# Split embedding weights kept in DRAM after the first pass, and new places for sums, transposes and loads, in a hybrid decoder step on one core

## The chip, the core and the metric

One Trainium2 chip, one core of it. The program works with five engines that each run their own list of instructions in order: TensorE (PE; PEld is its weight load), VectorE (DVE), ScalarE (ACT), GpSimd (POOL) and SyncE (SP), which here issues nearly every DMA. The metric is the device time of one execution in microseconds (us), as a median of several runs. Before the change it is 2644.22 us (three runs, 2639.54 to 2645.95).

## What is computed

One layer of a decoder for 2048 prompt tokens and 32 sample tokens (8 sequences of 4), all in float32, model width 1024:

```python
xn = rmsnorm(h, norm_mix);  proj = xn @ w_in                  # 1024 -> 3072, six groups of 512
o_a = rmsnorm(hgrn2_scan(...)) * silu(og)                     # 4 heads, 128x128 state each
z = conv31(ca * sigmoid(cg)) + bias                           # depthwise, 512 channels
o_b = silu(layernorm(z) * gain + bias)
h = h + concat(o_a, o_b) @ w_out
xn2 = rmsnorm(h, norm_ffn)
h = h + (silu(xn2 @ w_gate) * (xn2 @ w_up)) @ w_down          # inner width 2816
gate = sigmoid(rmsnorm(h, norm_ple) @ w_ple_gate)             # 1024 x 1024
h = h + gate * (p @ w_ple_proj)                               # 256 x 1024
y = rmsnorm(h, norm_final)
```

Outputs are y for prompt and sample, and the new scan and convolution states.

## The kernel before

**Numbers.** Every float32 matrix product is made of three TensorE products of a high and a low part: `wh*xl`, `wh*xh`, `wl*xh` (`mm3`, lines 541 to 544, and `mm3s`, 1630 to 1632). This text calls such three a triple. A weight piece of 128x512 is loaded as `raw`; ScalarE rounds it to `wh` (the helper `act`, shown as line 385), VectorE takes `wl = raw - wh` (the helper `tt`, line 390). `stt` (line 393) is the helper of operations with a scalar. Since helpers record them, nearly all VectorE rows carry lines 390 and 393 and are told apart by their tiles.

**Stages.** The mix stage (to about 945 us) goes over 8 blocks of 256 tokens: input norm, projections, scan, convolution, layer norm and output product, whose result h1 goes to DRAM (`h1d`). The second stage (`ffn`, 1920) goes over three passes of 696, 696 and 688 tokens, each of two halves (348 or 344 columns). A pass has 22 gate and up units `z` with Strassen's seven products for each (`strassen`, 1634; four of the seven weight combinations are kept in DRAM as `tch`/`tcl` by pass 0 and read by the others), six down stages `d`, and the embedding stage `p` (`embed`, 1863): 8 column tiles m with two weight pieces of the gate (`w_pg`) each and one piece of the projection (`w_pp`) for every two tiles. In the last pass the embedding goes over all eight tiles for half 0 and then again for half 1, so its pieces are loaded and split twice.

**Norms.** `rms2` (1287) makes a norm of one half: eight squares on ScalarE, eight sums on VectorE, one small memset (L1310), three transposes on TensorE (L1315), two reduces on VectorE (L1319, L1322), a power on GpSimd (`inverse_root`, shown as L426), and three transposes that spread the result (L1330). `norm2` is the norm before the ffn. Its `combine` (1371) takes the eight h1 columns of a pass two at a time per half (kp = 0 to 3): four loads and four scale operations, then the seven sums A12, A11, S1, A22, S2, S4, S3 that `strassen` multiplies with, in tiles `xa`/`x2`. kp = 3 ends last. `norm3` feeds the embedding together with `h2_split` (1935; tiles `xo`, `hx`), and `norm4` (1960) is the final norm: after its power, 16 scale operations (8 per half, L393 `h<-h,gn,px`) and the stores of y.

**Order.** `Sched.run` (188) writes all instructions in an order that it plans with estimated durations: for each engine the operation that can start first, then by a rank. A TensorE operation of any thread but the main ones (`lane`, `ffn`) that would have to wait is planned `SIDE` ns later, so that more products go ahead of it. Each engine, and SP's queue, then runs that list strictly in order on the chip. Buffers come from pools: `ring` (9 pairs of weight pieces, of which 4 hold the embedding's inputs, `pins`, through stage `p`), `raws`, `tmp2` (10 work tiles), `hres` (the residual of a pass), `main` (PSUM banks `pm`, with some `px`).

```python
                if e == "pe" and th[0].__name__ not in ("lane", "ffn") and s > self.clock[e]:
                    s += self.SIDE
```

## Time and profile before

| | |
|---|---|
| median of 3 runs | 2644.22 us |
| the profiled execution's own time | 2645.72 us |
| its span | 2644.0 us |
| mean granted TensorE clock | 0.98 of full speed |
| busy: PE / DVE / ACT / POOL | 96% / 75% / 41% / 5% |
| DMA: moved, mean rate | 470.86 MB, 178 GB/s |

The span is the time from the first to the last instruction; 1.7 us lie around it. A share of busy time is an average over the stages; where TensorE stands idle, and for whom, is read from its timeline and its waits. The granted clock has two levels, 1.00 (2.4 GHz) and 0.50 (1.2 GHz), and a stretch shows their mean.

### The profile page before, as it was taken

Reading aid. Unit: us, or ns where it says so; the run is one execution under the profiler, and the core shown is the slowest. Engines: PE = TensorE matmul, PEld = TensorE weight load, DVE = VectorE, ACT = ScalarE, POOL = GpSimd, SP = SyncE. Lnnn points to the kernel's source line nnn. Section 1 sums busy time; section 2 is a strip of 40 time slices with the busy share of each in tenths; the row PEclk is TensorE's granted clock in tenths of the full one; section 3 lists DMA queues with packets and bytes.
Section 4 is the critical chain, followed back from the end, with each engine's and each line's share of the span. In section 5 each row is a group of like instructions: output and inputs, shape, how many; then the busy total and the mean of one; then the engine's idle time right before and its main releaser. Section 6 shows DMA issues by size and latency. Waiting matters only on the chain.

```text
span 2644.0 us, 44170 instructions
## 1 busy us (share of the span) xinstructions
PE 2525.0 (96%) x15646; PEld 2368.0 (90%) x15646; DVE 1978.4 (75%) x4578; ACT 1082.1 (41%) x2477; POOL 140.4 (5%) x286
## 2 busy tenths in 40 slices
PE   7999999999999799999999899999998799999988
PEld 6987977778887699999999889999998799999977
DVE  8998899679886876666677857686587666677686
ACT  5553344334332343444354433343344334333353
POOL 0111010010110100000000000000000000000010
PEclk9999999999999799999999999999999899999999
DMA  8665646554546684565452374445622555554433
GB/s 310 222 211 187 236 159 199 197 179 162 165 139 204 201 278 164 187 211 177 159 207 74 128 255 169 154 161 192 216 81 96 163 193 195 196 173 162 148 95 118
DMA packets 290510, 470.86 MB, mean 178 GB/s; under 512 B 46576, under 2 KB 88048, under 8 KB 290288
## 3 DMA queue, kind: packets, MB, share of 16 engines
q1 hardware_dynamic: 287984, 466.63, 52.7%
q8 instruction: 123, 2.02, 0.3%
q10 hardware_dynamic: 2304, 1.41, 0.2%
q14 instruction: 99, 0.81, 0.1%
HBM read 368.27 MB, written 99.64 MB: 177 GB/s over the span
## 4 chain that ended last, share of the span: by engine, by line
PE 87%; DVE 6%; DMA 3%; POOL 1%; ACT 1%; issue 1%; SPq 0%; POOLq 0%; DVEq 0%; ACTq 0%
PE pm L1632 27%; PE px L1632 13%; PE pm L542 11%; PE pm L544 11%; PE pm L543 11%; PE px L544 2%; PE px L542 2%; PE px L543 2%; DVE h L390 1%; DVE wl L390 1%; PE pm L610 1%; PE pm L612 1%; PE pm L611 1%; DVE h L393 1%; POOL sm L426 1%
## 5 line engine op out<-in xcount | busy, mean ns | idle before, releaser
L390 DVE TENSOR_TENSOR wl<-raw,wh 128x512 fp32r<-128x512 f32 (+1 forms) x496 | 328.8, 667 | 151.8 <-ACT wh L385 138.9
L385 ACT ACTIVATE wh<-raw 128x512 fp32r<-128x512 f32 (+1 forms) x496 | 295.9, 608 | 309.4 <-PE pm L543 96.5
L542 PE MATMUL pm<-xal,wh 128*128 128x256 f32 (+2 forms) x960 | 324.0, 337 | 8.8 <-DVE xal L390 4.6
L544 PE MATMUL pm<-xah,wl 128*128 128x256 f32 (+2 forms) x960 | 311.1, 324 | 0.9 <-DMA wl<-wcl 0.9
L543 PE MATMUL pm<-xah,wh 128*128 128x256 f32 (+2 forms) x960 | 310.9, 324 | 0.0
L542 PE MATMUL pm<-xol,wh 128*128 128x348 f32 (+4 forms) x751 | 250.7, 334 | 9.2 <-ACT wh L385 5.2
L544 PE MATMUL pm<-xoh,wl 128*128 128x348 f32 (+4 forms) x751 | 246.4, 328 | 0.6 <-DVE wl L390 0.5
L543 PE MATMUL pm<-xoh,wh 128*128 128x348 f32 (+4 forms) x751 | 246.1, 328 | 0.0
L390 DVE TENSOR_TENSOR h<-pm,h 128x348 f32<-128x348 f32 (+1 forms) x335 | 172.5, 517 | 91.5 <-PE pm L544 42.6
L1632 PE MATMUL pm<-xal,wh 128*128 128x348 f32 (+1 forms) x707 | 228.6, 323 | 4.1 <-DVE h L390 1.8
L1632 PE MATMUL pm<-xah,wh 128*128 128x348 f32 (+1 forms) x707 | 227.6, 322 | 0.0
L1632 PE MATMUL pm<-xah,wl 128*128 128x348 f32 (+1 forms) x707 | 227.4, 322 | 0.1
L542 PEld LDWEIGHTS pm<-xal,wh 128*128 128x128 f32 x960 | 183.1, 191 | 36.0 <-issue 8.6
L393 DVE SCALAR_TENSOR_TENSOR t<-u,cvw,t 128x256 f32<-128x256 f32 x448 | 214.0, 478 | 0.0
L544 PEld LDWEIGHTS pm<-xah,wl 128*128 128x128 f32 x960 | 182.3, 190 | 15.8 <-DMA wl<-wcl 1.8
L385 ACT ACTIVATE wh<-tw 128x512 fp32r<-128x512 f32 x146 | 92.0, 630 | 249.7 <-DVE tw L390 92.9
L543 PEld LDWEIGHTS pm<-xah,wh 128*128 128x128 f32 x960 | 183.0, 191 | 11.7
L1632 PE MATMUL pm<-x2l,wh 128*128 128x348 f32 (+1 forms) x533 | 171.5, 322 | 6.1 <-DVE x2l L390 6.1
L426 POOL TENSOR_TENSOR sm<-sm,mhalf 128x2 f32<-128x2 f32 (+3 forms) x79 | 75.1, 952 | 1851.7 <-DVE sm L1322 1736.7
L393 DVE SCALAR_TENSOR_TENSOR h<-u,cvw,h 128x256 f32<-128x256 f32 x360 | 171.1, 476 | 2.2 <-ACT h L385 2.1
L1632 PE MATMUL pm<-x2h,wh 128*128 128x348 f32 (+1 forms) x533 | 171.7, 322 | 0.0
L1632 PE MATMUL pm<-x2h,wl 128*128 128x348 f32 (+1 forms) x533 | 171.7, 322 | 0.0
(292 smaller groups left out, 6513.7 us busy)
## 6 DMA issues: line engine op xcount, KB each, us to landing
raw<-w_gu SPq DMA_DIRECT2D x220, 256.0 KB, 3.2
wh<-wch SPq DMA_DIRECT2D x192, 256.0 KB, 2.8
wl<-wcl SPq DMA_DIRECT2D x192, 256.0 KB, 3.2
wh<-tch SPq DMA_DIRECT2D x176, 256.0 KB, 4.6
wl<-tcl SPq DMA_DIRECT2D x176, 256.0 KB, 4.8
raw<-w_dn SPq DMA_DIRECT2D x132, 256.0 KB, 3.2
tch<-wh SPq DMA_DIRECT2D x88, 256.0 KB, 2.8
tcl<-wl SPq DMA_DIRECT2D x88, 256.0 KB, 2.9
```

Source lines behind the costliest of these rows:

```text
L385: nc.scalar.activation(out, in_, func, scale=scale, bias=bias, **kw)
L390: return op("dve", d_tt(n), lambda: nc.vector.tensor_tensor(out=out, in0=a, in1=b, op=o), R, W)
L393: return op("dve", d_tt(n, not isinstance(s, float)), lambda: nc.vector.scalar_tensor_tensor(out=out, in0=a, scalar=s, in1=b, op0=o0, op1= ...
L426: return op("pool", 700.0, lambda: nc.gpsimd.tensor_tensor(out=s.ap[0:rows, out:out + n], in0=s.ap[0:rows, lo:lo + n], in1=mhalf[0:rows, 0 ...
L542: nc.tensor.matmul(out, lhsT=wh, rhs=xl, start=first, stop=False)
L543: nc.tensor.matmul(out, lhsT=wh, rhs=xh, start=False, stop=False)
L544: nc.tensor.matmul(out, lhsT=wl, rhs=xh, start=False, stop=last)
L610: nc.tensor.matmul(bank.ap, lhsT=xs[0], rhs=wl, start=(k == 0), stop=False)
L611: nc.tensor.matmul(bank.ap, lhsT=xs[0], rhs=wh, start=False, stop=False)
L612: nc.tensor.matmul(bank.ap, lhsT=xs[1], rhs=wh, start=False, stop=(k == KD - 1))
L1632: nc.tensor.matmul(out, lhsT=a, rhs=b, start=first and i == 0, stop=last and i == 2, skip_group_check=True)
```

## The change

1. **Kept embedding weights.** A new DRAM pair `pcache` (`pch`, `pcl`) has room for the 20 split pieces of stage `p`. In pass 0 each piece is split as before and then stored; passes 1 and 2 load the two parts from there into the ring pair instead of loading `raw` and splitting. `embed_tile` gives a pair back only after its store is issued. Passes 1 and 2 have 20 and 40 pieces.
2. **Final norm's transposes later.** `rms2` takes an event `late`, and `norm4` of passes 0 and 1 waits with its transposes until the next pass's first unit (half 0) or second unit (half 1) has its second product.
3. **Residual loads later.** `residual` for passes 1 and 2 starts after the second unit's second product.
4. **norm2 of the next pass earlier.** Its `combine` no longer waits for `norm3`'s rows.
5. **SIDE** becomes 4000 for norm2, norm3 and norm4, and stays 1000 for others.
6. **PN20** = 900 in place of 350: the rank of pass 0's norm2 and of its first two combines, whose work lies at the end of the mix stage beside the last block's convolution.

```diff
-    SIDE = 1000.0
+    SIDE = dict(norm2=4000.0, norm3=4000.0, norm4=4000.0)
...
-                    s += self.SIDE
+                    s += self.SIDE.get(th[0].__name__, 1000.0)
...
+    pcache = [dram.tile([20, 128, 512], F32, name="pc" + p) for p in "hl"]
...
     def residual():
         for t in PASSES:
+            if t:
+                yield wait(("zp", t, 0, 1, 1))
...
-    def rms2(n, get):
+    def rms2(n, get, late=None):
...
+        if late:
+            yield wait(late)
         bank = yield acq(misc)
...
     def norm2(t):
...
-            for h in HALVES:
-                yield wait(("r3", t - 1, h))
...
-            S.spawn(combine(t, kp, five), 350 if t == 0 and kp < 2 else 150 if t else 0)
+            S.spawn(combine(t, kp, five), PN20 if t == 0 and kp < 2 else 150 if t else 0)
...
-    S.spawn(norm2(0), 350)
+    S.spawn(norm2(0), PN20)
...
     def load2():
...
-                elif st[0] == "pin":
+                elif st[0] == "pin" or st[0] == "p" and t:
                     continue
...
+    def kept_name(key):
+        return key[:1] + key[2:-1]
+
+    def pkept(key):
+
+        at = 2 * key[2] + key[3] if key[0] == "p" else 2 * KD + key[2]
+        return [x[at] for x in pcache]
...
     def split2():
...
+                elif st[0] == "p" and t:
+                    for key, _ in plain(st, t):
+                        e = yield acq(ring)
+                        yield wait(("kept2", kept_name(key)))
+                        for x, part in zip(pkept(key), e):
+                            yield dma(part.ap.bitcast(F32), x, W=[part], nbytes=512 * 512)
+                        w2[key] = e
+                        S.fire(("w2", key))
...
+                        if st[0] == "p":
+                            S.spawn(keep_weights(pkept(key), e, ("kept2", kept_name(key))), 0)
...
     def embed_tile(t, m, hs):
...
         for a in range(2):
-            S.release(ring, w2.pop(("p", t, m, a, hs)))
+            key = ("p", t, m, a, hs)
+            yield wait(("kept2", kept_name(key)))
+            S.release(ring, w2.pop(key))
...
     def norm4(t, h):
         n = HALF[t]
-        bank = yield from rms2(n, of_res(t, h, "h3"))
+        bank = yield from rms2(n, of_res(t, h, "h3"), None if t == PASSES[-1] else ("zp", t + 1, 0, h, 1))
```

The new lines shift the helpers: in the orders of the change below, sums are line 392, scalar operations 395, `rms2`'s transposes 1321 and 1336, `mm3` 544 to 546, `mm3s` 1654 and the layer norm's last transposes 976.

**TensorE at the change from pass 0 to pass 1.** `px_181<-xah` (before) and `px_182<-xal` (now) are the first products of the new pass, `x2l` with them is the fourth column pair (kp = 3), `idn,f` and `idn,h` the final norm's first transposes, `idn,sm` the second ones. Before:

```order
L1632 MATMUL px_181<-xah,wl_81 128x348
L1315 MATMUL px_179<-idn,f_9125 128x128 x2
L1315 MATMUL px_179<-idn,f_9125 92x128
...
L1315 MATMUL px_182<-idn,f_9123 128x128 x2
...
L1330 MATMUL px_179<-idn,sm_67 128x128 x2
...
L1330 MATMUL px_182<-idn,sm_71 128x128 x2
...
L1632 MATMUL px_181<-x2l,wh_80 128x348
```

Now:

```order
L1654 MATMUL px_182<-xah,wl_81 128x348
L1654 MATMUL px_182<-x2l,wh_80 128x348
...
L1654 MATMUL pm_178<-x2l,wh_84 128x348
...
L1321 MATMUL px_183<-idn,h_77 128x128 x2
L1321 MATMUL px_183<-idn,h_77 92x128
L1654 MATMUL pm_180<-xal,wh_86 128x348
```

Before, both halves of the final norm stood ahead of the first product with kp = 3. Now that product follows the first three directly, and the transposes of half 0 come after the second group of four triples (six triples lie between its two transposes); half 1 follows in the second unit.

**VectorE at the same place.** `gn,r` are combine's scale operations, `gn,px` the final norm's 16, `x2l<-` the low parts of the sums of kp = 3; in the second excerpt `h_77,px_184`, `h_78` and `wl` belong to the embedding that ends (its last result, its residual sums, its last weights) and to the first weights of the new pass. Before:

```order
L393 SCALAR_TENSOR_TENSOR f_9124<-f_9124,gn,r_116 128x348
L393 SCALAR_TENSOR_TENSOR h_77<-h_77,gn,r_116 128x348
...
L393 SCALAR_TENSOR_TENSOR h_76<-h_76,gn,px_179 128x348 x3
L393 SCALAR_TENSOR_TENSOR h_79<-h_79,gn,px_179 128x348 x2
L393 SCALAR_TENSOR_TENSOR h_78<-h_78,gn,px_179 128x348 x3
L393 SCALAR_TENSOR_TENSOR h_76<-h_76,gn,px_182 128x348 x2
L393 SCALAR_TENSOR_TENSOR h_79<-h_79,gn,px_182 128x348 x3
L393 SCALAR_TENSOR_TENSOR h_78<-h_78,gn,px_182 128x348 x3
L390 TENSOR_TENSOR x2l<-f_9127,x2h 128x348
L390 TENSOR_TENSOR x2l<-h_77,x2h 128x348
```

Now:

```order
L395 SCALAR_TENSOR_TENSOR h_77<-h_77,px_184 128x348
L392 TENSOR_TENSOR wl_93<-raw_98,wh_92 128x512
L395 SCALAR_TENSOR_TENSOR h_78<-h_77,h_78 128x348
L392 TENSOR_TENSOR wl_97<-raw_102,wh_96 128x512
L395 SCALAR_TENSOR_TENSOR h_77<-h_77,gn,r_117 128x348
L392 TENSOR_TENSOR h_77<-h_77 128x348 x2
...
L392 TENSOR_TENSOR x2l<-h_77,x2h 128x348
...
L395 SCALAR_TENSOR_TENSOR h_76<-h_76,gn,px_181 128x348 x3
L395 SCALAR_TENSOR_TENSOR h_79<-h_79,gn,px_181 128x348 x2
L395 SCALAR_TENSOR_TENSOR h_78<-h_78,gn,px_181 128x348 x3
L392 TENSOR_TENSOR x2l<-h_77,x2h 128x348
```

Before, all 16 final scale operations stood between combine's last scale operation and A12 of kp = 3 (`x2l<-f_9127`). Now A12 (the first `x2l<-h_77`) comes ahead of them, seven VectorE instructions behind the embedding's last result (`h_77,px_184`), and eight of them stand ahead of S2 (`x2l<-h_77` at the end), which TensorE's fourth group of products needs. The same change of order is at the change from pass 1 to 2, where now all of kp = 3 but one sum is ahead of the last embedding operations.

**TensorE at the end of the mix stage.** `t` and `h_78` belong to the last block's scan and layer norm, `idn,h_77` and `idn,sm` to norm2 of pass 0, `pm<-xol` is the first output product. Before:

```order
L1205 MATMUL px_179<-idn,t_155 128x128 x2
L1207 MATMUL px_179<-idn,t_153 128x32
L1315 MATMUL px_179<-idn,h_77 128x128 x2
...
L1330 MATMUL px_180<-idn,sm_69 128x128 x2
...
L974 MATMUL px_179<-idn,h_78 128x128 x2
L974 MATMUL px_179<-idn,u_148 128x32
...
L974 MATMUL px_181<-idn,u_149 128x32
L542 MATMUL pm_177<-xol,wh_96 128x256
```

Now:

```order
L1209 MATMUL px_181<-idn,t_155 128x32
L1321 MATMUL px_182<-idn,h_77 128x128 x2
...
L1336 MATMUL px_181<-idn,sm_69 128x128 x2
...
L976 MATMUL px_184<-idn,h_78 128x128 x2
L976 MATMUL px_184<-idn,u_150 128x32
...
L976 MATMUL px_181<-idn,u_151 128x32
L1321 MATMUL px_184<-idn,h_77 128x128 x2
...
L1336 MATMUL px_182<-idn,sm_74 128x128 x2
...
L544 MATMUL pm_179<-xol,wh_96 128x256
```

Before, the transposes of norm2's half 0 came earlier, between the scan's products, and half 1's ahead of the layer norm's second set (`idn,h_78`, `idn,u`). Now half 0 is there, and half 1 stands between that set and the first output product.

## Rows read from the trace of the kernel before

**Rows 1.** The profile's page, busy time of each engine.
```profile
PE 2525.0 (96%) x15646; PEld 2368.0 (90%) x15646; DVE 1978.4 (75%) x4578; ACT 1082.1 (41%) x2477; POOL 140.4 (5%) x286
```

**Rows 2.** Stretches: busy us (instructions) per engine, granted clock, DMA share, GB/s.
```profile
1995.00:2075.00 80.00, 78.92 (x482) 78.50 (x481) 62.91 (x132) 36.26 (x76) 0.85 (x1) 0.97 0.35 114
2078.00:2104.00 26.00, 16.25 (x65) 14.63 (x66) 18.04 (x42) 5.86 (x13) 2.78 (x2) 0.67 0.55 165
20.00:30.00 10.00, 9.44 (x60) 8.35 (x60) 7.92 (x25) 5.53 (x16) 0.70 (x1) 1.00 1.06 405
```

**Rows 3.** Waits of TensorE: total us, times, longest us.
```profile
PE px L1330 <- POOL sm L426: 23.2, 9, 5.6
```

**Rows 4.** TensorE in time, change from pass 0 to 1: start, us, ..., [idle before].
```profile
1507.64 0.32 PE L1632 MATMUL px<-xah,wl 128*128 128x348 f32 x1
1511.17 0.99 PE L1315 MATMUL px<-idn,f 128*128 128x128 f32 x6 [3.21 <-DVE sm L1310]
1513.90 1.66 PE L1330 MATMUL px<-idn,sm 128*128 128x128 f32 x6 [1.74 <-POOL sm L426]
1526.18 0.66 PE L1632 MATMUL px<-x2l,wh 128*128 128x348 f32 x1 [10.62 <-DVE x2l L390]
```

**Rows 5.** VectorE in time, the same place.
```profile
1506.63 0.52 DVE L393 SCALAR_TENSOR_TENSOR f<-f,px 128x348 f32<-128x348 f32 x1 [0.43 <-PE px L544]
...
1517.81 7.88 DVE L393 SCALAR_TENSOR_TENSOR h<-h,gn,px 128x348 f32<-128x348 f32 x16
1525.61 0.52 DVE L390 TENSOR_TENSOR x2l<-f,x2h 128x348 fp32r<-128x348 f32 x1
```

**Rows 6.** TensorE in time, change from pass 1 to 2.
```profile
2078.70 0.90 PE L1315 MATMUL px<-idn,f 128*128 128x128 f32 x3 [4.51 <-DVE sm L1310]
...
2083.27 0.84 PE L1330 MATMUL px<-idn,sm 128*128 128x128 f32 x3 [2.59 <-POOL sm L426]
...
2096.78 0.66 PE L1632 MATMUL pm<-x2l,wh 128*128 128x344 f32 x1 [6.06 <-DVE x2l L390]
...
2119.55 0.55 PE L1632 MATMUL px<-xal,wh 128*128 128x344 f32 x1 [2.44 <-DMA wh<-tch]
```

**Rows 7.** TensorE in time, start of pass 1's embedding.
```profile
1990.70 0.84 PE L1330 MATMUL px<-idn,sm 128*128 128x128 f32 x3 [5.63 <-POOL sm L426]
1994.14 0.66 PE L542 MATMUL pm<-xol,wh 128*128 128x348 f32 x1 [2.59 <-ACT wh L385]
```

**Rows 8.** GpSimd in time, the same place.
```profile
1985.17 5.48 POOL L426 TENSOR_TENSOR sm<-sm,mhalf 128x3 f32<-128x3 f32 x1 [192.69 <-DVE sm L1322]
2001.94 0.85 POOL L426 TENSOR_TENSOR sm<-sm,mhalf 128x3 f32<-128x3 f32 x1 [11.29 <-DVE sm L1322]
```

**Rows 9.** VectorE in time, the same place.
```profile
1984.95 1.05 DVE L393 SCALAR_TENSOR_TENSOR xol<-h,gn,xoh 128x348 fp32r<-128x348 f32 x2
...
1988.88 1.06 DVE L393 SCALAR_TENSOR_TENSOR xol<-h,gn,xoh 128x348 fp32r<-128x348 f32 x2
```

**Rows 10.** TensorE in time, start of pass 2's embedding.
```profile
2549.32 0.84 PE L1330 MATMUL px<-idn,sm 128*128 128x128 f32 x3 [5.61 <-POOL sm L426]
2552.74 0.66 PE L542 MATMUL pm<-xol,wh 128*128 128x344 f32 x1 [2.58 <-ACT wh L385]
```

**Rows 11.** TensorE in time, end of the mix stage.
```profile
892.55 0.90 PE L1315 MATMUL px<-idn,h 128*128 128x128 f32 x3 [0.59 <-ACT hg L385]
897.41 0.84 PE L1330 MATMUL px<-idn,sm 128*128 128x128 f32 x3 [3.96 <-POOL sm L426]
```

**Rows 12.** VectorE in time, the same place.
```profile
898.78 0.58 DVE L393 SCALAR_TENSOR_TENSOR h<-h,gn,r 128x348 f32<-128x348 f32 x1 [0.61 <-ACT r L385]
```

**Rows 13.** Groups on VectorE, 1995 to 2075 us: count | busy, mean ns | idle.
```profile
L390 DVE TENSOR_TENSOR wl<-raw,wh 128x512 fp32r<-128x512 f32 x23 | 15.7, 689 | 5.5 <-ACT wh L385 5.5
```

**Rows 14.** Groups on ScalarE, 1995 to 2075 us.
```profile
L385 ACT ACTIVATE wh<-raw 128x512 fp32r<-128x512 f32 x21 | 13.0, 627 | 19.5 <-PE pm L543 11.8 <-issue 4.9 <-PE px L543 2.0
```

**Rows 15.** DMA issues of the page: count, KB each, median us to landing.
```profile
wh<-tch SPq DMA_DIRECT2D x176, 256.0 KB, 4.6
```

More of the change, by code (lines that the diff above doesn't have):

```diff
@@ L63 @@
 PSQ = 0
+PN20 = 900
 RANK = {"o": -2.0}
@@ L1901, in embed_tile @@
         if m % 2:
-            S.release(ring, w2.pop(("pp", t, m // 2, hs)))
+            key = ("pp", t, m // 2, hs)
+            yield wait(("kept2", kept_name(key)))
+            S.release(ring, w2.pop(key))
     def embed_evac(t, m, h, gate, proj):
```

## The prediction

> **What bounds the kernel now.** I read the page's busy shares first, where only TensorE is near full, 96% [rows 1], then stretches of the trace, then the waits of TensorE, then its timeline wherever it stops. In the middle of a pass's embedding TensorE works 78.92 of 80 us at a granted clock of 0.97 [rows 2], while VectorE and ScalarE have air: TensorE sets the time there, and work taken off the others is worth nothing by itself. Time is to be had only where TensorE stands. Its waits name the second transposes of a norm, for the power on GpSimd: 23.2 us in nine waits, 5.6 the longest [rows 3]. The timeline puts these waits, and longer ones, at the seams. From pass 0 to 1 it stands 3.21, 1.74 and 10.62 us, the last for VectorE's low part of a sum [rows 4]; VectorE was then in sixteen final scale operations, 7.88 us long, ahead of that sum [rows 5]. From pass 1 to 2 it stands 4.51, 2.59 and 6.06 us, and 2.44 for a weight load [rows 6]. At the start of the embedding of pass 1 it stands 5.63 us for the power and 2.59 for ScalarE's rounding of a weight [rows 7], at that of pass 2 5.61 and 2.58 [rows 10]. At the end of the mix stage it stands 3.96 us for a power [rows 11]. Each stop also brings the clock down: 2078 to 2104 us has a mean of 0.67 [rows 2].
>
> **The change part by part.** The sum is made against the profiled execution's own 2645.7 us (2644.0 of span and 1.7 around it), which is 1.5 above the median of the runs.
>
> *Split pieces no longer made (60 of them).* Each saves VectorE 0.689 us [rows 13] and ScalarE 0.627 [rows 14], some 40 and 38 us in all. TensorE is full there, so this counts nothing. If that cover were gone, only the four waits of the two embedding starts would show it. In place of the raw loads come 120 part loads, and 40 stores in pass 0. In pass 2 a tile of one half has ten triples of products; 482 instructions in 78.92 us [rows 2] are 0.164 each, so a tile takes 4.9 us and needs 2.5 pieces of two 256 KB parts, 1.31 MB, or 267 GB/s. The core has moved 405 GB/s in a stretch [rows 2]. Nothing is added for it; the bound above is rival 3. The added wait of `embed_tile` for the kept copy stands behind stores issued some us after the split, while the pair is still in use: nothing.
>
> *First weights of the embedding.* Passes 1 and 2 no longer wait for ScalarE's rounding: −2.59 and −2.58 [rows 7, 10]. The parts can be loaded long before, since half of the ring is free by then. Between norm3's first and second transposes now stand four triples in pass 1 and five in pass 2 instead of three; they fill 0.5 and 1.0 us of the waits of 5.63 and 5.61. The rest of these waits I leave: the power itself took 5.48 us [rows 8] beside ten VectorE operations that run from 1984.95 to 1989.94 [rows 9], and 0.85 where VectorE was quiet [rows 8]; in the new order nine of the ten still follow the norm's reduces. Sum of the two places −6.7; bounds 0 (a late load takes the rounding's place) and −16 (the powers go at 0.85 too).
>
> Here a rule and a row part. The Trainium skill, page "SBUF — State Buffer", section "Who interferes with whom", says that an operation of VectorE with two SBUF inputs and a GpSimd operation that reads SBUF exclude each other, and that the loser blocks until the other's instruction is finished. By that rule the power would lose one operation and then go, and the wait would not depend on how many follow. The trace disagrees: the power ended only with the series. By the row the two waits stay, by the rule they would go with any change of order; that is rival 2.
>
> *Pass 0 to 1.* The three waits, 15.6 us, go: the first product with kp = 3 no longer stands behind both halves of the final norm. Next in line is A12 itself. Behind the embedding's last result, which VectorE took at 1506.63 [rows 5], stand seven operations; with the durations of [rows 5, 12, 13] these are 0.52 + 0.69 + 0.52 + 0.69 + 0.58 + 1.04 + 0.52 = 4.6 us, with starts overlapping by 0.05 a piece as the sixteen do (7.88/16 = 0.49 [rows 5]) about 4.2, so A12 is there at 1510.9. TensorE wants it behind its third triple, at 1507.8 [rows 4]: a new wait of 3.1. The second is S2, which TensorE wants one triple after norm4's second transposes while VectorE starts eight scale operations then: 8 × 0.49 + 0.5 for the sum's low part − 0.5 to 0.9 for that triple, about 3.6. Norm4's chain from its first transposes to its second takes 4.9 − 0.9 = 4.0 us [rows 11]; six triples cover 2.9, the remaining 1 and the second half's like wait fall into these two. Each stop costs half-clock products behind it: 2 more. −15.6 + 3.1 + 3.6 + 2 = −6.9; bounds −15.6 (the scale operations move behind S2's need) and 0 (the sums come so late that TensorE stops as long as before).
>
> *Pass 1 to 2.* Here the order has all but one sum of kp = 3 ahead of the last embedding operations. Gone: 4.51 + 2.59 + 6.06 [rows 6], and 2.44 for the weight load, since the residual's loads that were queued ahead of it start two units later: 15.6. The half clock: 26 us at a mean of 0.67 hold 17.2 at half speed [rows 2]; the three stops there take 13.2 of the 26, so between 4.0 and 12.8 us of work went at half speed and cost 2.0 to 6.4; I take 4, the middle. Against it norm4's chain of 4.0 beside 2.9 of products, for two halves: between 0 and 2.2, taken as 1.5. −15.6 − 4 + 1.5 = −18.1; bounds −20 and −9.
>
> *End of the mix stage.* Half 1 of norm2 now has its whole chain between the layer norm's last transposes and the first output product, with no product in between. One such chain runs from 892.55 to 898.25, 5.7 us [rows 11]; half 0 takes the place half 1 had. Combine, which began at 898.78 [rows 12], begins some 8 us later; its sums then leave the front of the last convolution's VectorE work, at 0.5 each. I take +6, the chain alone; bounds 0 (the sums given back pay for it) and +12 (two chains in series).
>
> Residual loads later, and `SIDE`, have no term beyond these places. Sum: −6.7 − 6.9 − 18.1 + 6 = −25.7, so 2620.0 on the profile's scale and **2618.5** on the median's.
>
> **The rivals.** *1. The seams give little.* Pass 0 to 1 gains nothing (S2 takes the place of A12), the mix end costs its upper bound of 12, pass 1 to 2 keeps its weight wait of 2.44 and half of the clock's share, 14, and a load eats 1.7 of the embedding starts' gain, 5: 0 + 12 − 14 − 5 = −7, 2637. For it: eight scale operations do stand ahead of S2, and the norm's chain is longer than the products laid over it. Against it: at the change to pass 2 the order is clean. That the change doesn't do what it says, as to TensorE's order, is part of this. *2. The powers go quickly.* If one VectorE operation is all that holds a power up, or the new order leaves a hole for it, it takes 0.5 + 0.85 = 1.4 us in place of 5.48, and with the products between the transposes 4.5 more are won at each of two places: 2618.5 − 9 = 2609. Against it stand [rows 8, 9]. *3. Slower: the ring starves in pass 2.* Four of nine pairs hold the embedding's inputs, so five circulate in the first half of pass 2, two tiles' worth. A pair given back must be filled within about 2 × 4.9 = 9.8 us; from a landing of 9.8 on TensorE stops every two tiles, four times in eight tiles, by what is over. The loads of kept parts in the ffn land in 4.6 (median) [rows 15]. At a landing of 19.3 the four stops are 38 us: 2656, slower than before. It needs four times the landing seen; stores of y in the same queue speak a little for it.
>
> **How the numbers follow.** Forecast 0.65, rival 1 0.18, rival 2 0.12, rival 3 0.05. A measurement of this kernel tells some 0.3% from no change, 7.9 us, 2636.3 to 2652.1. The forecast's own terms run from about −45 to −5 at their ends together, but not all at one end; I give it 2607 to 2632. With rival 2 the range reaches down to 2600, with rival 1 up to 2637. Faster: forecast, rival 2 and half of rival 1, which lies at the bound: 0.65 + 0.12 + 0.08 = 0.85; same: the rest of rival 1, 0.10; slower: 0.05.
>
> **What would show it.** Right: TensorE's waits for `x2l` at the change to pass 1 are two of some 3 us instead of one of 10.6; at the change to pass 2 no wait over 2 us; no wait of the embedding's first product for ScalarE, but still 4.5 to 5.2 for the power; a first output product some 6 us later at the end of the mix stage. Wrong: a wait on `wh` or `wl` for a DMA within the embedding of pass 2 (rival 3); a power under 2 us at an embedding's start (rival 2); a wait of 7 us or more for S2 (rival 1).

## The result, and the profile after

The changed kernel takes 2628.84 us (median of 4 runs, 2628.53 to 2631.96) beside 2645.01 of the kernel before (4 runs). The ratio is 0.9946, interval 0.9929 to 0.9963: faster by 0.5%, some 14 us (16 by the two medians). The forecast was 2618.5 within 2600 to 2637, so sign and range hold, and the gain is little more than half of the 26 us that were summed. The profiled execution has a span of 2630.2 us, 13.8 shorter than before.

The page of the changed kernel, busy time of each engine, against [rows 1]:

```profile
PE 2525.8 (96%) x15646; PEld 2371.2 (90%) x15646; DVE 1938.9 (74%) x4518; ACT 1048.0 (40%) x2417; POOL 136.8 (5%) x286
```

TensorE is as busy as before; what changed is idle time and clock. Its waits (total us, times, longest us) beside [rows 3]:

```profile
PE px L1336 <- POOL sm L428: 16.3, 6, 4.4
...
PE pm L544 <- DVE h L392: 7.8, 1, 7.8
...
PE pm L1654 <- DVE x2l L392: 4.4, 1, 4.4
...
PE px L1654 <- DVE x2l L392: 4.2, 1, 4.2
PE pm L1654 <- DMA wh<-tch: 4.2, 1, 4.2
```

The one wait of 10.6 us for `x2l` is two of 4.4 and 4.2, as was expected (at 3.6 and 3.1). The waits for a norm's power sank from 23.2 us in nine to 16.3 in six. A wait of 7.8 for an output product's bank and one of 4.2 for a kept weight part are new in size. Two stretches (busy us and count of PE, PEld, DVE, ACT, POOL; granted clock; DMA share; GB/s):

```profile
2078.00:2104.00 26.00, 26.00 (x171) 25.92 (x171) 19.82 (x45) 9.53 (x19) 1.70 (x2) 1.00 0.83 269
1500.00:1550.00 50.00, 41.45 (x232) 40.68 (x232) 34.37 (x75) 17.60 (x37) 1.49 (x1) 0.86 0.61 199
```

The stretch 2078 to 2104 us, which had 16.25 us of products at a clock of 0.67 [rows 2], is now full at 1.00. The change from pass 0 to 1 still has holes.

To place the gain, the trace is cut at instructions that every version has: the first gate product, the last embedding product of pass 0, the first and the last product of the embeddings of passes 1 and 2, the last instruction of TensorE. Times in us:

| stretch | before | changed | difference | in the forecast |
|---|---|---|---|---|
| start to first gate product | 959.30 | 970.28 | +11.0 | +6 |
| pass 0 to its last embedding product | 547.23 | 547.18 | −0.1 | 0 |
| from there to pass 1's embedding | 475.55 | 470.27 | −5.3 | −6.9 |
| pass 1's embedding | 90.71 | 90.73 | 0.0 | −3.1 |
| from there to pass 2's embedding | 467.94 | 454.05 | −13.9 | −18.1 |
| pass 2's embedding | 89.36 | 83.63 | −5.7 | −3.6 |
| tail | 6.14 | 6.08 | −0.1 | 0 |
| sum | 2636.24 | 2622.22 | −14.0 | −25.7 |

How far such a stretch differs between traces of the same order is seen from the experiments below: the first one is 959.3, 959.8, 957.4, 962.0 and 958.3 us in the five versions with the old order at the mix stage's end, and 965.4 to 971.6 in the nine with the new one, means 959.4 and 968.3. So by the traces the new order costs some 9 us there, and 2 or 3 of the 11 lie within what one trace differs from another.

**The change from pass 0 to 1,** on TensorE and (second fence) on VectorE, beside [rows 4, 5]; the columns are start, us, engine, line, operation, tiles, shape, count and, in brackets, the idle time before and what ended it:

```profile
1523.06 0.66 PE L1654 MATMUL px<-x2l,wh 128*128 128x348 f32 x1 [4.16 <-DVE x2l L392]
...
1536.44 0.66 PE L1654 MATMUL pm<-x2l,wh 128*128 128x348 f32 x1 [4.39 <-DVE x2l L392]
```

```profile
1518.71 0.51 DVE L395 SCALAR_TENSOR_TENSOR h<-h,px 128x348 f32<-128x348 f32 x1
...
1522.49 0.51 DVE L392 TENSOR_TENSOR x2l<-h,x2h 128x348 fp32r<-128x348 f32 x1
...
1531.97 3.98 DVE L395 SCALAR_TENSOR_TENSOR h<-h,gn,px 128x348 f32<-128x348 f32 x8
1535.87 0.51 DVE L392 TENSOR_TENSOR x2l<-h,x2h 128x348 fp32r<-128x348 f32 x1
```

The embedding's last result is taken at 1518.71, A12's low part at 1522.49, and TensorE starts with it at 1523.06 after 4.16 us. Then eight final scale operations take 3.98 us, S2's low part comes right behind them at 1535.87, and TensorE goes on at 1536.44 after 4.39. Both waits are those of the forecast (3.1 and 3.6), by the same rows of VectorE. The last scale operation ahead of A12 started at 1521.00, as its load landed (1520.97), so the place of the loads bounds it too (experiment 9).

**The embedding of pass 1,** TensorE, GpSimd and VectorE, beside [rows 7 to 9]:

```profile
1996.52 0.84 PE L1336 MATMUL px<-idn,sm 128*128 128x128 f32 x3 [3.39 <-POOL sm L428]
...
2011.78 0.51 PE L1336 MATMUL px<-idn,sm 128*128 128x128 f32 x3 [2.09 <-POOL sm L428]
```

```profile
1991.50 4.96 POOL L428 TENSOR_TENSOR sm<-sm,mhalf 128x3 f32<-128x3 f32 x1 [194.08 <-DVE sm L1328]
2009.48 2.25 POOL L428 TENSOR_TENSOR sm<-sm,mhalf 128x3 f32<-128x3 f32 x1 [13.02 <-DVE sm L1328]
```

```profile
1994.69 1.06 DVE L395 SCALAR_TENSOR_TENSOR xol<-h,gn,xoh 128x348 fp32r<-128x348 f32 x2
...
2007.78 0.58 DVE L395 SCALAR_TENSOR_TENSOR f<-f,gn,r 128x344 f32<-128x344 f32 x1 [3.24 <-DMA f<-h1d]
2008.27 0.41 DVE L1325 TENSOR_REDUCE sm<-px 128x2 f32<-128x256 f32 x1
...
2009.03 0.28 DVE L1328 TENSOR_REDUCE sm<-px 92x1 f32<-92x128 f32 x1
...
2010.51 0.50 DVE L392 TENSOR_TENSOR h<-h,f 128x344 f32<-128x344 f32 x1
```

No product waits for ScalarE's rounding here any more; the first one waits 0.63 us for its kept part, the third 0.57. The wait for the power of the first half is 3.39 us in place of 5.63, but there is now a second wait for a power, 2.09 us, for the norm's second half. Behind it stand two rows of VectorE: a scale operation of combine for the next pass waited 3.24 us for its load, with the reduces of the norm (2008.27, 2009.03) queued behind it; and the sums of that combine ran beside the power, which took 2.25 us in place of 0.85.

**The change from pass 1 to 2,** first SyncE's queue (issues of one kind in a row are one line: start, us, count), then TensorE, beside [rows 6]:

```profile
2089.36 5.06 SPq L473 DMA_DIRECT2D y<-h  x9
2094.53 0.40 SPq L473 DMA_DIRECT2D raw<-w_gu  x1
2095.02 4.26 SPq L473 DMA_DIRECT2D y<-h  x9
...
2117.25 2.88 SPq L473 DMA_DIRECT2D y<-h  x6
...
2122.20 0.43 SPq L473 DMA_DIRECT2D wh<-tch  x1
```

```profile
2127.22 0.65 PE L1654 MATMUL pm<-xal,wh 128*128 128x344 f32 x1 [4.15 <-DMA wh<-tch]
```

All waits of the old order for VectorE and GpSimd are gone, the one for the weight load is not: 4.15 us in place of 2.44. From 2089 to 2122 us the queue issues 40 stores of y in eight groups, which take it 19.8 us (three of the groups are shown), some 0.5 each; a part issued at 2122.20 is what lands when TensorE's wait ends.

The same stretch has a second new wait at its far end, and the embedding of pass 2 behind it one for the power that is shorter than before (5.61 [rows 10]); TensorE:

```profile
2528.06 0.53 PE L1654 MATMUL pm<-xol,wh 128*128 128x344 f32 x1 [2.22 <-DVE h L392]
...
2540.02 0.51 PE L1336 MATMUL px<-idn,sm 128*128 128x128 f32 x3 [3.00 <-POOL sm L428]
```

The wait of 2.22 us, in the last down stage, is for a bank that VectorE empties at 2527.50, behind the low parts of the embedding's inputs. It is there, with 2.2 to 2.3 us, in every version with kept embedding weights and in none without them.

**The end of the mix stage,** TensorE and VectorE, beside [rows 11, 12]:

```profile
896.52 0.84 PE L1336 MATMUL px<-idn,sm 128*128 128x128 f32 x3 [4.41 <-POOL sm L428]
...
905.51 0.88 PE L1321 MATMUL px<-idn,h 128*128 128x128 f32 x3 [4.91 <-DVE sm L1314]
908.03 0.84 PE L1336 MATMUL px<-idn,sm 128*128 128x128 f32 x3 [1.64 <-POOL sm L428]
...
933.52 0.58 PE L544 MATMUL pm<-xol,wh 128*128 128x256 f32 x1 [7.80 <-DVE h L392]
```

```profile
925.74 0.95 DVE L392 TENSOR_TENSOR xal<-h,xah 128x348 fp32r<-128x348 f32 x2 [0.56 <-ACT xah L387]
...
931.69 0.95 DVE L392 TENSOR_TENSOR xal<-h,xah 128x348 fp32r<-128x348 f32 x2 [0.56 <-ACT xah L387]
...
933.05 0.75 DVE L392 TENSOR_TENSOR h<-h,pm 128x256 f32<-128x256 f32 x2
```

Half 1's transposes wait 4.91 us more and its power 1.64, and then an output product waits 7.80 us (4.04 before) for a bank that `h<-h,pm` at 933.05 has to empty. That operation stands in VectorE's list behind combine's second set of sums (925.74 to 932.64), which now begin later.

### The profile page after: what moved, and what is told of

The parts are those of the page before. It is cut to its first block, busy times and chain, and to the rows that moved or that the text cites. A ratio compares the mean times of both kernels' runs of the same rounds, so it can differ in the third digit from the quotient of the medians.

```text
span 2630.2 us, 44193 instructions
## 1 busy us (share of the span) xinstructions
PE 2525.8 (96%) x15646; PEld 2371.2 (90%) x15646; DVE 1938.9 (74%) x4518; ACT 1048.0 (40%) x2417; POOL 136.8 (5%) x286
## 4 chain that ended last, share of the span: by engine, by line
PE 87%; DVE 5%; DMA 4%; ACT 2%; POOL 1%; issue 1%; SPq 0%; POOLq 0%; DVEq 0%; ACTq 0%
PE pm L1654 28%; PE px L1654 12%; PE pm L544 11%; PE pm L546 10%; PE pm L545 10%; PE px L546 2%; PE px L544 2%; PE px L545 2%; DVE h L392 1%; PE pm L612 1%; PE pm L614 1%; PE pm L613 1%; DMA wl<-wcl 1%; DVE wl L392 1%; PE px L1136 1%; DMA h<-h1d 1%
## 5 line engine op out<-in xcount | busy, mean ns | idle before, releaser
L392 DVE TENSOR_TENSOR wl<-raw,wh 128x512 fp32r<-128x512 f32 (+1 forms) x436 | 287.6, 663 | 148.0 <-ACT wh L387 142.2
L387 ACT ACTIVATE wh<-raw 128x512 fp32r<-128x512 f32 (+1 forms) x436 | 258.9, 606 | 276.7 <-PE pm L545 90.6
L544 PE MATMUL pm<-xol,wh 128*128 128x348 f32 (+4 forms) x721 | 240.8, 334 | 8.4 <-DVE h L392 7.8
L1654 PE MATMUL pm<-xal,wh 128*128 128x348 f32 (+1 forms) x734 | 238.2, 325 | 9.2 <-DMA wh<-tch 4.2
L546 PE MATMUL pm<-xoh,wl 128*128 128x348 f32 (+4 forms) x721 | 236.6, 328 | 1.3 <-DMA wl<-pcl 1.3
L1654 PE MATMUL pm<-xah,wl 128*128 128x348 f32 (+1 forms) x734 | 236.8, 323 | 0.0
L545 PE MATMUL pm<-xoh,wh 128*128 128x348 f32 (+4 forms) x721 | 236.3, 328 | 0.0
L1654 PE MATMUL pm<-x2l,wh 128*128 128x348 f32 (+1 forms) x566 | 182.7, 323 | 4.4 <-DVE x2l L392 4.4
L1654 PE MATMUL pm<-x2h,wh 128*128 128x348 f32 (+1 forms) x566 | 182.9, 323 | 0.0
L1654 PE MATMUL pm<-x2h,wl 128*128 128x348 f32 (+1 forms) x566 | 182.6, 323 | 0.0
```

Of the source, the lines that this page charges most:

```text
L387: nc.scalar.activation(out, in_, func, scale=scale, bias=bias, **kw)
L392: return op("dve", d_tt(n), lambda: nc.vector.tensor_tensor(out=out, in0=a, in1=b, op=o), R, W)
L544: nc.tensor.matmul(out, lhsT=wh, rhs=xl, start=first, stop=False)
L545: nc.tensor.matmul(out, lhsT=wh, rhs=xh, start=False, stop=False)
L546: nc.tensor.matmul(out, lhsT=wl, rhs=xh, start=False, stop=last)
L1654: nc.tensor.matmul(out, lhsT=a, rhs=b, start=first and i == 0, stop=last and i == 2, skip_group_check=True)
```

## The experiments

All times are medians; a ratio is against runs of the kernel before on the same chip (medians 2645.97 to 2646.83).

**1. The old order at the end of the mix stage.**

```diff
-PN20 = 900
+PN20 = 350
-    SIDE = dict(norm2=4000.0, norm3=4000.0, norm4=4000.0)
+    SIDE = dict(norm3=4000.0, norm4=4000.0)
```

> The changed kernel with PN20 = 350 and norm2's SIDE at 1000, so that the end of the mix stage has the order that it had before; all else as changed. Theory: the first gate and up product came 11.0 us later after the change (970.28 against 959.30 us), and all of that is this order; the wait of 7.80 us for an output product's bank falls to some 4, and the kernel to 2617 to 2619 us. Rival: the later start of combine bought something behind it, in pass 0; then the first product is back at 959 but the time falls by under 6 us, to 2623 or more.

2625.64 us, ratio 0.9923 (0.9910 to 0.9937), against 0.9946 of the changed kernel: some 6 us by the ratios and 3 by the medians, less than expected and a time that the rival named. TensorE there:

```profile
896.84 0.84 PE L1336 MATMUL px<-idn,sm 128*128 128x128 f32 x3 [3.94 <-POOL sm L428]
...
923.35 0.39 PE L544 MATMUL pm<-xol,wh 128*128 128x256 f32 x1 [4.31 <-DVE h L392]
```

The bank wait is back at 4.31, and the first gate product at 959.80, 10.5 us earlier. Pass 0 is no longer than before (546.70), so nothing was bought there; the stretches behind pass 0 are 4.2 us longer together, 0.5 to 1.5 each, although every engine's order is the same there. So the rival's reason falls: the later start of combine bought nothing in pass 0, and behind it nothing is ordered otherwise. The price of part 6 and of norm2's part of part 5 is 9 us by the traces' first stretch and 3 to 6 by the times; that it is a price and no gain is shown, its size only so far.

**2. norm4's scale operations behind S3.**

```diff
         bank = yield from rms2(n, of_res(t, h, "h3"), ...)
+        if t != PASSES[-1]:
+            yield wait(("x2", t + 1, KP - 1, "S3"))
         for m in range(KD):
```

> The changed kernel, in which norm4 of passes 0 and 1 holds its sixteen scale operations back until the last sum (S3) of kp = 3 is made. Theory: the second wait at the change from pass 0 to 1 (4.39 us, for S2's low part) is the eight scale operations ahead of it on VectorE; it falls under 1.5 us, the first (4.16, A12) stays, and the kernel takes 2623 to 2625 us. Rival: S2 is late because the whole chain of sums behind A12 is late; the wait stays over 3 us and the time at 2627 to 2630.

2623.18 us, ratio 0.9919 (0.9905 to 0.9933), a time that the theory named, and the wait that it named:

```profile
1520.12 0.66 PE L1654 MATMUL px<-x2l,wh 128*128 128x348 f32 x1 [4.50 <-DVE x2l L392]
...
1530.10 0.43 PE L1654 MATMUL pm<-x2l,wh 128*128 128x348 f32 x1 [0.51 <-DVE x2l L392]
```

The A12 wait stays (4.50), the S2 wait is 0.51. In this trace the stretch to pass 1's embedding is 470.21 us, no shorter than the changed kernel's 470.27: a wait of 2.25 us for a weight part comes at 1570. Sixteen stores of y are issued until 1546.4 there, with TensorE 3 us ahead, and until 1539.8 in the changed kernel; that they make this load late was not tested. The place of the S2 wait is shown. Where the 5 us of the medians come from is not: in the trace 2.4 us lie in the first stretch, whose order is that of the changed kernel, 1.2 in pass 1's embedding and 1.1 on the way to pass 2's.

**3. The stores of y on ScalarE's queue.**

```diff
-            if t == PASSES[-1] and m % 2:
+            if t != PASSES[-1] or m % 2:
```

> The changed kernel, in which the stores of y of passes 0 and 1 are issued by ScalarE's queue instead of SyncE's. Theory: the wait of 4.15 us for a kept weight part early in pass 2 (2127 us) is SyncE's queue: stores of y, 0.43 us each to issue, stand ahead of the weight loads; without them the wait falls under 1 us and the kernel takes 2623 to 2625 us. Rival: the load is late in the memory, or behind residual loads; the wait stays over 3 us and the time at 2627 to 2631.

2647.55 us, ratio 1.0007 (0.9998 to 1.0016): the whole gain is lost, 8.7 us of it on the way to pass 1's embedding and 7.3 on the way to pass 2's. The wait for the weight part is gone, and this has come in its place, on TensorE and on ScalarE (ACTq is its queue):

```profile
2113.64 0.66 PE L1654 MATMUL pm<-xal,wh 128*128 128x344 f32 x1 [8.10 <-ACT h L387]
```

```profile
2103.45 4.77 ACTq L2003 DMA_DIRECT2D y<-h  x6
2108.26 0.46 ACT L387 ACTIVATE f<-px 128x344 f32<-128x344 f32 x1 [4.26 <-DMA y<-h]
2108.82 4.26 ACTq L2003 DMA_DIRECT2D y<-h  x6
2113.12 0.46 ACT L387 ACTIVATE h<-pm 128x344 f32<-128x344 f32 x1 [4.41 <-DMA y<-h]
```

An issue holds ScalarE's list some 0.4 us, and longer where the store waits for its data; single activations, which TensorE waits for, stand between groups of six. The miss says how costly these stores are where they stand in one burst, but not yet that they are what made the load late on SyncE.

**4. norm2 waits for norm3's rows again (part 4 undone).**

```diff
                     yield wait(("pin", t - 1, k, h))
+            for h in HALVES:
+                yield wait(("r3", t - 1, h))
```

> The changed kernel, in which norm2 of passes 1 and 2 waits again for norm3's rows (part 4 of the change undone). Theory: in the embedding of pass 1 the wait of 2.09 us for the second half's power goes, since no operation of combine waits for its load ahead of the norm's reduces, and the embedding gets 2 to 4 us shorter; at the change from pass 1 to 2 the sums of kp = 3 are late again, a wait of 4 to 7 us; together 2627 to 2634 us. Rival: the early start buys nothing at that change; then only the gain is seen, 2624 to 2626.

2629.45 us, ratio 0.9943 (0.9930 to 0.9956), the same as the changed kernel, by two opposite effects. The embedding of pass 1 is 85.29 us long (90.73), with no second wait for the power: 5.4 us won. Against it, at the change from pass 0 to 1:

```profile
1526.45 0.66 PE L1656 MATMUL px<-x2l,wh 128*128 128x348 f32 x1 [11.04 <-DVE x2l L392]
```

the A12 wait is back at 11.04 and that stretch 3.5 us longer; the one to pass 2 is 2.2 longer. So part 4 takes 7 us off the wait for A12 at the first change of pass and gives 5.4 back in the next embedding. The expectation named the second change for the loss; it was the first.

**5. Without kept weights (part 1 undone).** The raw pieces of passes 1 and 2 are loaded and split as before; the stores, the part loads and the two waits for kept copies are taken out.

```diff
-                elif st[0] == "pin" or st[0] == "p" and t:
+                elif st[0] == "pin":
...
-                        if st[0] == "p":
-                            S.spawn(keep_weights(pkept(key), e, ("kept2", kept_name(key))), 0)
```

> The changed kernel without the kept embedding weights (part 1 undone): raw pieces are loaded and split again in passes 1 and 2. Theory: TensorE gains from part 1 only at the two embedding starts, where it waited 2.6 us each for ScalarE's rounding; these waits and their half clock come back, nothing else moves: 2634 to 2637 us, with some 40 us more of VectorE and ScalarE work hidden. Rival 1: the freed VectorE and ScalarE also shorten the rest of the embedding; then 2640 us or more. Rival 2: the kept parts' double loads cost as much as the splits; then 2627 to 2631.

2628.33 us, ratio 0.9933 (0.9921 to 0.9946): no slower than the changed kernel. The number is the second rival's, its reason is not. Pass 2's embedding gets 5.0 us longer (88.60), as the theory had it, but not for its reason. No wait for ScalarE's rounding comes back at either embedding's start; the power's wait there is 7.40 us in pass 1 and this, on TensorE and GpSimd, in pass 2, in place of 3.00:

```profile
2533.52 0.84 PE L1336 MATMUL px<-idn,sm 128*128 128x128 f32 x3 [7.33 <-POOL sm L428]
```

```profile
2526.35 7.12 POOL L428 TENSOR_TENSOR sm<-sm,mhalf 128x3 f32<-128x3 f32 x1 [431.75 <-DVE sm L1328]
```

In this order the low parts of the embedding's inputs follow directly on the ten operations that ran beside the power before, and the power ended 0.7 us behind the last of all fourteen. Pass 1's embedding is 2.2 us shorter all the same (88.50), without a second wait for a power. The way to pass 2's embedding is 9.5 us longer (463.55), with sums late for the new pass:

```profile
2070.51 0.66 PE L1644 MATMUL pm<-x2l,wh 128*128 128x344 f32 x1 [9.42 <-DVE x2l L392]
```

But the stretch from pass 0 to pass 1's embedding takes 456.88 us in place of 470.27, with no wait over 0.7 us at the change of pass. Something in part 1 costs 13 us there, and no part is loaded yet at that change of pass: new up to it are only the 40 stores and the ring pairs' wait for them.

**6. Without `late` (part 2 undone).**

```diff
-        bank = yield from rms2(n, of_res(t, h, "h3"), None if t == PASSES[-1] else ("zp", t + 1, 0, h, 1))
+        bank = yield from rms2(n, of_res(t, h, "h3"), None)
```

> The changed kernel without the event `late` (part 2 undone): norm4's transposes of passes 0 and 1 stand where SIDE alone puts them, behind the first four triples of the new pass, the two halves close together. Theory: SIDE alone already takes the waits for the norm from the front of the pass; without `late` all sixteen scale operations come together ahead of S2, whose wait of 4.39 us at the change from pass 0 to 1 becomes 7 to 9: 2632 to 2636 us. Rival: `late` is the whole gain at the two changes of pass; then 10.6 and 6.1 us waits are back and the time is 2640 us or more.

2633.53 us, ratio 0.9948 (0.9934 to 0.9961). By the median 4.7 us more than the changed kernel, by the ratios the same; the traces decide:

```profile
1523.45 0.66 PE L1654 MATMUL px<-x2l,wh 128*128 128x348 f32 x1 [3.93 <-DVE x2l L392]
...
1541.33 0.66 PE L1654 MATMUL pm<-x2l,wh 128*128 128x348 f32 x1 [7.84 <-DVE x2l L392]
```

The wait for S2 is 7.84 (4.39 with `late`), that stretch 5.5 us longer, and no wait for the norm's transposes is back. `SIDE` alone moves them; `late` keeps the second half's eight operations out of S2's way. The theory stands for the place of the wait; for the size of the loss only the medians and the trace speak.

**7. The stores of y spread over four units.**

```diff
         r = res[t, m, h]
+        if t != PASSES[-1]:
+            at_ = 8 * h + m
+            yield wait(("zp", t + 1, 0 if at_ < 12 else 1, (1 + at_ // 4) % 4, (0, 2, 3, 5)[m % 4]))
```

> The changed kernel, in which the stores of y of passes 0 and 1 stay on SyncE's queue but wait for products of the second to fifth unit of the next pass, four columns in each, in place of being issued at once. Theory: the burst of stores ahead of weight loads is what makes the load at 2127 us late (ScalarE's queue only moved the burst to where it held up activations); paced, the wait of 4.15 us falls under 1.5 us and no new wait comes: 2622 to 2626 us. Rival: the queue has no room for them in the later units either; another wait for a weight load of 2 us or more comes behind, 2627 to 2632 us.

2622.10 us, ratio 0.9907 (0.9894 to 0.9921): SyncE issues them in groups of two to six with weight loads between,

```profile
2092.23 3.15 SPq L473 DMA_DIRECT2D y<-h  x6
...
2099.32 3.49 SPq L473 DMA_DIRECT2D y<-h  x6
```

and no wait for a weight load over 0.7 us is left at that change; the stretch to pass 2's embedding is 445.83 us, 8.2 shorter. The order of every engine but SyncE's is that of the changed kernel, instruction for instruction, so nothing else was changed: the load was late for the burst of stores in its queue.

**8. Experiments 1, 2 and 4 (this for pass 2 alone) together.**

> The changed kernel with three edits together: the old order at the end of the mix stage (as in the first experiment), the scale operations of norm4 behind S3 (as in the second), and norm2 of pass 2 alone waiting for norm3's rows (as in the fourth, but not for pass 1, where that brought a wait of 11 us). Theory: the three places are apart and add up: 6 to 9 us, 5 to 6 and about 3 off 2628.8, so 2611 to 2615 us. Rival: what one gives another takes back at the next change of pass; 2617 to 2622 us.

2615.63 us, ratio 0.9881 (0.9866 to 0.9895), just above the range that the sum gave; the first stretch is 957.35 us, the embedding of pass 1 85.24. The wait of 4.29 for A12 and one of 3.23 for the weight part are still there.

**9. The planner counts no bytes for the 40 stores.** The stores are made as before.

```diff
-    def keep_weights(kept, parts, ev):
+    def keep_weights(kept, parts, ev, nbytes=512 * 512):
...
-            yield dma(c, t.ap.bitcast(F32), R=[t], nbytes=512 * 512)
+            yield dma(c, t.ap.bitcast(F32), R=[t], nbytes=nbytes)
...
-                            S.spawn(keep_weights(pkept(key), e, ("kept2", kept_name(key))), 0)
+                            S.spawn(keep_weights(pkept(key), e, ("kept2", kept_name(key)), 0), 0)
```

> The changed kernel, in which the planner counts no bytes for the 40 stores of kept embedding weights in pass 0; the stores themselves are made as before. Theory: without kept weights (fifth experiment) pass 0 to 1 took 456.9 us from the end of the embedding to the next one, with them 470.3, since the planner, which counts the stores' transfer time ahead of combine's loads, put combine's sums of kp = 3 later in VectorE's and ScalarE's lists; the chip has room for the stores. Then that stretch is 457 to 460 us, the waits of 4.16 and 4.39 us go, the rest stays as in the changed kernel: 2615 to 2619 us. Rival: the stores hold the loads up on the chip too; then combine's operations wait for their loads in the new order, the stretch stays at 466 or more and the time at 2625 to 2632.

2620.43 us, ratio 0.9902 (0.9888 to 0.9917). The stretch from pass 0 to 1's embedding is 458.96 us and the waits of 4.16 and 4.39 are gone, with the same stores on the same queue. So it was the plan: it keeps one clock for all transfers and moves it on by the bytes of each, and with the stores' bytes ahead of combine's loads it put the sums of kp = 3 behind the embedding's last operations. The four loads of kp = 3 are issued at 1496.8 to 1504.4 us here, where the embedding's last product ends at 1519.2, and at 1510.4 to 1516.3 in the changed kernel, where it ends at 1517.5. The chip pays a little for the stores: pass 0 is 3.7 us longer (550.85), with waits for the powers of that embedding that the changed kernel didn't have (the second is 1.05):

```profile
1444.24 0.51 PE L1336 MATMUL px<-idn,sm 128*128 128x128 f32 x3 [0.89 <-POOL sm L428]
```

**10. Experiments 1, 7 and 9 together.**

> The ninth experiment's kernel with the old order at the end of the mix stage (first experiment) and the paced stores of y (seventh). Theory: three places that are apart; off 2628.8 come 11 to 13, 6 to 9 and 6 to 8: 2599 to 2606 us. Rival: they overlap at the change from pass 0 to 1, where the stores of y and combine's loads share a queue: 2608 to 2613.

2604.84 us, ratio 0.9846 (0.9831 to 0.9860): the three places add up, 24 us below the changed kernel and some 41 below the kernel before. Both changes of pass lie in full stretches at full clock:

```profile
1500.00:1550.00 50.00, 50.00 (x320) 49.92 (x319) 40.26 (x87) 22.21 (x48) 1.70 (x2) 1.00 0.78 252
2050.00:2100.00 50.00, 50.00 (x323) 49.92 (x322) 38.94 (x84) 21.98 (x45) 1.70 (x2) 1.00 0.79 256
```

**11. The same, with norm2 of pass 2 behind norm3's rows.**

> The tenth experiment's kernel, in which norm2 of pass 2 waits for norm3's rows again. Theory: as in the fourth and eighth, the embedding of pass 1 gets some 5 us shorter (no second wait for the power), and the change to pass 2 some 2 us longer: 3 under the tenth. Rival: with the stores of y out of the way combine's sums are what bounds that change, and it gets 5 us longer: no gain over the tenth.

2606.67 us, ratio 0.9856 (0.9839 to 0.9873): no gain that can be told. The embedding of pass 1 is 4.3 us shorter (85.71 against 90.05), the way to pass 2's 7.0 longer (453.09 against 446.06), as the rival had it: once the stores are out of the way, the sums bound that change.

**12. Residual loads early again (part 3 undone).**

```diff
-            if t:
-                yield wait(("zp", t, 0, 1, 1))
```

> The changed kernel, in which the residual loads of passes 1 and 2 start again as soon as their buffers come free (part 3 undone). Theory: a residual load needs the buffer that a store of y gives back, so the burst of stores spaces these loads out by itself; the wait for a weight part at the change from pass 1 to 2 stays at 3 to 5 us and the time at 2627 to 2631 us. Rival: part 3 does hold that wait down; without it weight loads come later still, another 3 us or more of waits early in passes 1 and 2: 2632 to 2637.

2630.17 us, ratio 0.9935 (0.9919 to 0.9951), the same; the wait for the weight part is 5.26. Part 3 does nothing that these runs can tell.

## Why the prediction was right, and half of it wrong

The reading held that TensorE sets the time and gains only at the seams: its busy time is unchanged, and VectorE's 40 and ScalarE's 34 us less are nowhere in the table. Right were the waits that go, and the two that take their place from pass 0 to 1 (4.16 and 4.39 against 3.1 and 3.6; −5.3 against −6.9). Three terms were mis-sized, and the cause of one that came out right was not seen. Of the signs that the prediction named, two failed: a wait over 2 us at the change to pass 2, 4.15, and the waits for the power at the embeddings' starts, 3.39 and 3.00 in place of 4.5 to 5.2.

*End of the mix stage, +6.* By the traces +9 (+11.0 in the one above), by the times 3 to 6. I counted the chain of norm2's half 1; the operation that empties an output bank, queued behind combine's sums and so later by as much as they are, was not in it (7.80 us against 4.04 before, 4.31 in experiment 1).

*"2.44 for the weight load, since the residual's loads that were queued ahead of it start two units later."* The load was behind the stores of y; it became 4.15 (experiments 7 and 12). In experiment 7 the stretch is 8.2 us shorter without this wait, more than the whole difference between −13.9 and −18.1. The wait of 2.22 us in the last down stage was in no term either.

*First weights of the embedding, −3.1 and −3.6.* Pass 2 gave −5.7, pass 1 nothing. The wait for ScalarE is gone in both, but in experiment 5 it is gone without kept weights too, so part 1 was not needed for that. In pass 2 more came off the power's wait than I had counted: eight operations in place of ten ran beside the power, which took 4.43 us in place of 5.41, and five triples stood over it, the first of them at half clock. In pass 1 part 4 lets combine run into the embedding, ahead of the norm's reduces (experiment 4: 85.29 us without it). I had read part 4 only for what it gives at the change of pass, not for what it is put in front of.

*"Nothing is added for it"* (part 1's 40 stores and 120 part loads). I priced the bytes on the chip, which has room for most of them. But the planner prices them too, and by its book the stores came ahead of combine's loads, so it put later what TensorE needs first: 470.27 us against 456.88 without part 1 and 458.96 with the stores uncounted. The two waits from pass 0 to 1, which I took as the price of part 2's place for the norm, come with part 1: in experiments 5 and 9 both are gone (there the plan also puts the norm's half 0 some triples later). In the sum this was no miss, since I read the two waits from an order that already held them; I had the right size from the wrong cause.

Of the rivals, the first (the seams give little) came nearer than the forecast in three of its four terms: 12 for the mix stage's end, 14 for pass 1 to 2 and 5 for the embeddings' starts, against 11.0, 13.9 and 5.7 in the table. Only its nothing from pass 0 to 1 was wrong. The measured time lies between the two, 10 us above the forecast and 8 under that rival's 2637, near the slow end of the 2607 to 2632 that the forecast's own terms were given.

The second was that the powers go quickly: they did not. Each ended with the series of VectorE operations beside it: at 1996.46 where the series ended at 1995.75, at 2011.73 where it ended at 2011.01, 0.7 us behind it both times. By the rule of the Trainium skill (page "SBUF — State Buffer", section "Who interferes with whom") the loser of the shared port blocks until the other's instruction is finished. Read as one instruction, this is not what these traces show: 4.96 us went by with nine of them. The third, a starving ring, did not come: the longest wait for a kept part in pass 2's embedding is 0.76 us, and the parts land in 3.5 and 3.8 us.

What stays open: why stretches differ between traces of the same order, by up to 6 us in the first one (965.4 to 971.6) and by 1 to 2 in the others, and so how the 3 us and more between times and traces in experiment 1 come about; and which part of the change took the waits for ScalarE's rounding away.

## What to carry to other kernels

In a kernel whose order is planned ahead, every transfer that is added is paid twice, on the chip and in the planner's book; where the chip has room but the book has none, the work that waits for later loads moves, and the price appears in another stage. When a wait is removed so that work can start earlier, look at what this work is put in front of on each engine's list, its own loads above all. And a burst of small stores delays the loads queued behind it: spread it, and keep it off an engine that computes.

## What the runs showed of the hardware

A store issued from ScalarE's queue takes its list 0.4 us and more (six in 2.81 to 4.77 us, experiment 3), nearly the time of an activation there (0.46); on SyncE it is about 0.5 (six in 2.88 us, nine in 4.26 and 5.06). A GpSimd power beside VectorE operations with two inputs in SBUF ended 0.7 us behind the last of the series, whatever its length: 7.12 us beside fourteen (experiment 5), 4.96 beside nine, 4.43 beside eight, 2.25 beside four, 0.85 alone. A VectorE operation with one input in PSUM right behind the fourteen did not prolong it.
